# A sum of reciprocals on one core: every other early load issued by ScalarE, and fewer waits on VectorE

## The chip, the cores and the metric

One core of a Trainium2 chip. The metric is the time of one execution in device microseconds (us), as a median over several runs, with the kernel before measured beside each new one on the same chip. All runs compared here are undisturbed (fast). SyncE and ScalarE issue the loads; TensorE, VectorE, ScalarE and GpSimd (POOL in the profile) compute.

## The reference

```python
x = np.abs(np.random.randn(32, 512, 1024)).astype(np.float32) + 1e-6
return np.sum(1.0 / x, axis=-1).astype(np.float32)
```

That is 16,384 rows of 1024 numbers, 128 rows on each of 128 partitions, 67.11 MB to read and almost nothing to write. In what follows "row" means one row on each partition.

## The kernel before

The kernel never divides a single number. It splits each row in halves a and b and uses 1/a + 1/b = (a + b) / (a b). A product a b is made on GpSimd or, for some rows, on VectorE with b copied to PSUM by TensorE. ScalarE turns it into its reciprocal with Ln and Exp. VectorE multiplies by the other factor and sums: either over the whole row with the reciprocal broadcast, or over the sum a + b, which TensorE has made. Rows come in chunks of two, of three kinds `(rows, rows whose a + b TensorE makes, rows whose product VectorE makes)`:

```python
A, B, C = (2, 0, 0), (2, 2, 0), (2, 2, 1)
LOADS = [[A, B, A, C]] * 10 + [[A, B], [A, C]] * 4 + [[A], [B], [A], [C]] * 2
...
ppool = ctx.enter_context(tc.tile_pool(name="ppool", bufs=6))
...
def sum_row(c, row, fac):
    i = nc.vector.tensor_tensor_reduce(
        out=row, in0=row, in1=fac, scale=S, scalar=0.0, op0=mult, op1=plus,
        accum_out=sums[:, c : c + 1],
    )
...
for chunks in LOADS:
    n = sum(m for m, _, _ in chunks)
    xt = ring[:, c0 % R : c0 % R + n, :]                      # ring of R = 40 rows
    keep(nc.sync.dma_start(out=xt, in_=x_v[:, c0 : c0 + n, :]))
    # ... VectorE's products of this load
    # ... per chunk: GpSimd's product, TensorE's a + b,
    #     VectorE's sums of the chunk before, ScalarE's Ln and Exp
```

So the first ten loads have eight rows (4 MB) each, eight have four rows and eight have two. Each load needs ring rows that VectorE has done with.

## Time and profile before

| | |
|---|---|
| time before | 172.55 us (172.23 to 172.75, 4 runs) |
| span of the profiled run | 170.5 us |
| loads | 67.11 MB, near 425 GB/s from the second slice to the 37th |
| busiest engines | TensorE 80%, ScalarE 78%, GpSimd 78% |

The row of the DMA engines is full, the engines are not. One reads such a page by asking next how late each engine runs behind the loads, because the time ends with the last row's way through all of them. The lines for it are in the prediction.

### The profile page before, as it was taken

How to read it: one execution, taken by the hardware profiler on the slowest of the kernel's cores; microseconds unless marked ns; L12 is line 12 of the kernel's file. 1: busy time of each engine (PE TensorE's matmuls, PEld its weight loads, DVE VectorE, ACT ScalarE, POOL GpSimd, SP SyncE). 2: the span in 40 equal slices, each digit the busy share in tenths (PEclk: the TensorE clock that was granted, in tenths of full speed). 3: DMA queues.
4: the chain of work that ended last, by engine and by line, in shares of the span. 5: the costliest groups of instructions: out<-in, count | busy, mean ns of one | idle time of the engine just before them, and what ended most of it. 6: DMA issues, size and time to landing. Idle time of an engine off the chain costs nothing.

```text
span 170.5 us, 1320 instructions
## 1 busy us (share of the span) xinstructions
PE 136.0 (80%) x288; PEld 52.7 (31%) x288; DVE 124.9 (73%) x272; ACT 133.5 (78%) x129; POOL 133.0 (78%) x70
## 2 busy tenths in 40 slices
PE   0008999988889888786988887979999998896790
PEld 0003444332332333242333323323434332332240
DVE  0001778777987777787777769888998988889683
ACT  3002979979787997959799797899999988999790
POOL 1008969696996969589696969999999799996930
PEclk9999999999999999999999999999999999999999
DMA  6999999999999999999999999999999999999300
GB/s 208 415 446 431 438 423 446 415 454 423 448 423 431 431 438 419 431 432 423 446 415 446 423 404 427 431 423 431 427 427 423 427 413 423 421 421 419 146 0 15
DMA packets 3895, 67.25 MB, mean 394 GB/s; under 512 B 432, under 2 KB 560, under 8 KB 560
## 3 DMA queue, kind: packets, MB, share of 16 engines
q1 hardware_dynamic: 3888, 67.18, 92.7%
q8 instruction: 2, 0.03, 0.1%
q14 instruction: 5, 0.04, 0.1%
HBM read 67.11 MB, written 0.07 MB: 394 GB/s over the span
## 4 chain that ended last, share of the span: by engine, by line
DMA 66%; POOL 23%; issue 6%; DVE 1%; ACT 1%; DVEq 0%; POOLq 0%
DMA ring<-in_x_dram 66%; POOL pr L136 23%; DVE ring L92 1%; ACT pr L147 1%; ACT rc L151 1%; DVE pr L92 0%; DVEq L190 0%; POOLq L136 0%; DVE sums L92 0%; DVEq L92 0%
## 5 line engine op out<-in xcount | busy, mean ns | idle before, releaser
L136 POOL TENSOR_TENSOR pr<-ring 128x1024 f32<-128x1024 f32 x64 | 132.3, 2099 | 29.9 <-DMA ring<-in_x_dram 29.7
L82 PE MATMUL s<-ring,ident 128*128 128x512 f32 x256 | 121.2, 612 | 14.7 <-DVE sums L92 13.0
L92 DVE CUSTOM_DVE_ANT_1 ring<-ring,rc 128x1024 f32<-128x1024 f32 x64 | 75.6, 1219 | 26.2 <-ACT rc L151 22.2
L147 ACT ACTIVATE pr<-pr 128x1024 f32<-128x1024 f32 x64 | 67.3, 1051 | 30.0 <-POOL pr L136 29.7
L82 PEld LDWEIGHTS s<-ring,ident 128*128 128x128 f32 x256 | 47.4, 193 | 86.6 <-issue 49.4
L92 DVE CUSTOM_DVE_ANT_0 pr<-pr,s 128x512 f32<-128x512 f32 x64 | 41.4, 683 | 0.8 <-ACT pr L157 0.7
L157 ACT ACTIVATE pr<-pr 128x1024 f32<-128x1024 f32 x32 | 33.8, 1057 | 1.0
L151 ACT ACTIVATE rc<-pr 128x1024 f32<-128x1024 f32 x32 | 32.9, 1028 | 1.0
L82 PE MATMUL b<-ring,ident 128*128 128x512 f32 x32 | 18.5, 662 | 16.0 <-DMA ring<-in_x_dram 15.8
L125 DVE TENSOR_TENSOR pr<-ring,b 128x512 f32<-128x512 f32 x16 | 10.9, 684 | 16.1 <-PE b L82 16.0
L82 PEld LDWEIGHTS b<-ring,ident 128*128 128x128 f32 x32 | 5.3, 196 | 26.6 <-issue 15.4
L92 DVE DVE_READ_ACCUMULATOR2_ANT sums<- 128x1 f32 x128 | 10.6, 83 | 0.0
L53 ACT ACT_TABLE_LOAD x1 | 1.3, 1283 | 0.7 <-PEq L179 0.7
masks.py:197 POOL MEMSET ident<- 128x128 f32 x1 | 0.2, 204 | 0.3 <-POOLq L179 0.3
masks.py:199 POOL TENSOR_SCALAR_AFFINE_SELECT ident<-ident 128x128 f32<-128x128 f32 x1 | 0.3, 292 | 0.1
L179 POOL MEMSET const-float32-0.0<- 128x1 f32 x1 | 0.1, 98 | 0.2 <-issue 0.2
L179 POOL MEMSET const-bfloat16-1.0<- 128x1 bf16 x1 | 0.1, 101 | 0.0
L179 POOL MEMSET const-uint8-127<- 128x1 uint8 x1 | 0.1, 101 | 0.0
L179 POOL MEMSET const-float32-1.0<- 128x1 f32 x1 | 0.1, 98 | 0.0
## 6 DMA issues: line engine op xcount, KB each, us to landing
ring<-in_x_dram SPq DMA_DIRECT2D x10, 4096.0 KB, 37.7
ring<-in_x_dram SPq DMA_DIRECT2D x8, 2048.0 KB, 36.7
ring<-in_x_dram SPq DMA_DIRECT2D x8, 1024.0 KB, 28.2
out_dram<-sums SPq DMA_DIRECT2D x1, 64.0 KB, 1.5
```

What stands on the lines that cost most here:

```text
L53: nc.scalar.add_instruction(mybir.InstLoadActFuncSet(name=nc.get_next_instruction_name(), act_func_set_id=act_sets.index("natural_log_exp_ ...
L82: i = nc.tensor.matmul(bank, lhsT=ident, rhs=half, start=k == 0, stop=k == len(halves) - 1,)
L92: i = nc.vector.tensor_tensor_reduce(out=row, in0=row, in1=fac, scale=S, scalar=0.0, op0=mult, op1=plus, accum_out=sums[:, c : c + 1],)
L125: i = nc.vector.tensor_tensor(out=pr[:, j, :], in0=xt[:, q + j, :H], in1=b, op=mult)
L136: i = nc.gpsimd.tensor_tensor(out=pr[:, v:, :], in0=xc[:, v:, :H], in1=xc[:, v:, H:], op=mult)
L147: keep(nc.scalar.activation(out=pr, in_=pr, func=Ln, scale=S))
L151: i = nc.scalar.activation(out=rc, in_=pr[:, e:, :], func=Exp, scale=-1.0)
L157: keep(nc.scalar.activation(out=r, in_=r, func=Exp, scale=-1.0))
L179: nc = _bacc.Bacc("TRN2", target_bir_lowering=False, num_devices=1)
```

## The change

It has three parts. The loads 1, 3, 5, 7 and 9 are issued by ScalarE: two at the start, the others three loads ahead of the chunk that ScalarE is at. Every second of the ten big loads is A,B,A,B in place of A,B,A,C, which drops five products on VectorE and gives those rows to GpSimd. And VectorE is to wait less: the first sum of an A chunk writes its by-product to pr (the tile that holds the products) in place of the ring, the two rows of a B or C chunk are summed in reverse order, and pr gets two tags of four buffers.

```diff
-    LOADS = [[A, B, A, C]] * 10 + [[A, B], [A, C]] * 4 + [[A], [B], [A], [C]] * 2
+    LOADS = [[A, B, A, B], [A, B, A, C]] * 5 + [[A, B], [A, C]] * 4 + [[A], [B], [A], [C]] * 2
-    ppool = ctx.enter_context(tc.tile_pool(name="ppool", bufs=6))
+    ppool = ctx.enter_context(tc.tile_pool(name="ppool", bufs=4))
-    def sum_row(c, row, fac):
+    def sum_row(c, row, fac, out=None):
-            out=row,
+            out=row if out is None else out,
         # ... in sum_rows, for the rows of an A chunk:
+                pr[:, e : e + 2, :] if j == e and m - e > 1 else None,
-        for j in range(e):
+        for j in reversed(range(e)):
         # ... per load k, with AHEAD, OTHER = 3, 10:
-        keep(nc.sync.dma_start(out=xt, in_=x_v[:, c0 : c0 + n, :]))
+        ahead = range(k, k + AHEAD + 1) if k == 0 else (k + AHEAD,)
+        for a in ahead:
+            if a < OTHER and a % 2:
+                load(nc.scalar, a)
+        if k >= OTHER or k % 2 == 0:
+            load(nc.sync, k)
-            pr = ppool.tile([P, m, H], f32, tag="pr")
+            pr = ppool.tile([P, m, H], f32, tag="ps" if e else "pr")
```

More of the change, by code (lines that the diff above doesn't have):

```diff
@@ L33 @@
     F = 128
+    AHEAD, OTHER = 3, 10
     R = 40
@@ L107, in sum_rows, with load @@
             row = xc[:, j, :].rearrange("p (h e) -> p h e", h=2)
-            sum_row(c + j, row, rc[:, j - e, :].unsqueeze(1).to_broadcast([P, 2, H]))
-        for j in range(e):
-            sum_row(c + j, pr[:, j, :], sm[j])
+            sum_row(
+                c + j,
+                row,
+                rc[:, j - e, :].unsqueeze(1).to_broadcast([P, 2, H]),
+                pr[:, e : e + 2, :] if j == e and m - e > 1 else None,
+            )
+        for j in reversed(range(e)):
+            sum_row(c + j, pr[:, j, :], sm[j])
+    first = [0]
+    for chunks in LOADS:
+        first.append(first[-1] + sum(m for m, _, _ in chunks))
+    def load(eng, a):
+        r0, n = first[a], first[a + 1] - first[a]
+        i = eng.dma_start(
+            out=ring[:, r0 % R : r0 % R + n, :], in_=x_v[:, r0 : r0 + n, :]
+        )
+        keep(i)
     waiting = None
     c0 = 0
-    for chunks in LOADS:
+    for k, chunks in enumerate(LOADS):
         n = sum(m for m, _, _ in chunks)
         xt = ring[:, c0 % R : c0 % R + n, :]
-        keep(nc.sync.dma_start(out=xt, in_=x_v[:, c0 : c0 + n, :]))
+        ahead = range(k, k + AHEAD + 1) if k == 0 else (k + AHEAD,)
[4 more added lines that the diff above has]
+            load(nc.sync, k)
         made, q = [], 0
         for m, e, v in chunks:
-            pr = ppool.tile([P, m, H], f32, tag="pr")
+            pr = ppool.tile([P, m, H], f32, tag="ps" if e else "pr")
             for j in range(v):
```

## The prediction

> **What bounds the kernel now.** I read the page's first two parts, to see which resource is never idle.
>
> ```profile
> PE 136.0 (80%) x288; PEld 52.7 (31%) x288; DVE 124.9 (73%) x272; ACT 133.5 (78%) x129; POOL 133.0 (78%) x70
> DMA  6999999999999999999999999999999999999300
> GB/s 208 415 446 431 438 423 446 415 454 423 448 423 431 431 438 419 431 432 423 446 415 446 423 404 427 431 423 431 427 427 423 427 413 423 421 421 419 146 0 15
> ```
>
> No engine is above 80%, and the DMA row stands at 9 from the second slice to the 37th, at some 425 GB/s. The loads are the bound as long as they are queued early enough. That is in the part on DMA issues:
>
> ```profile
> ring<-in_x_dram SPq DMA_DIRECT2D x10, 4096.0 KB, 37.7
> ```
>
> A load lands 37.7 us after its issue while one takes about 9.85 us (first waits below: (102.11 - 13.42) / 9 loads), so nearly four loads are always queued. VectorE, which frees the ring, has that much slack and cannot starve the queue.
>
> Next the chain that ended last, in order of time, for what becomes of the two ends:
>
> ```profile
> 0.74 12.68 DMA ring<-in_x_dram
> ...
> 13.49 8.24 POOL pr L136 x4
> ...
> 64.52 37.59 DMA ring<-in_x_dram
> ...
> 131.56 25.52 DMA ring<-in_x_dram
> ...
> 159.69 2.38 POOL pr L136
> 162.09 1.07 ACT pr L147
> 163.18 1.04 ACT rc L151
> 164.34 0.62 DVE ring L92
> ```
>
> Load 0 lands at 13.42, load 9 at 102.11 (64.52 + 37.59). After the last loads a row goes through GpSimd's product, ScalarE's Ln and Exp and VectorE's sums; the output leaves at 167.95 and the span ends at 170.5. Last, the timeline of GpSimd alone, whose rows give start, length, and the wait before it:
>
> ```profile
> 23.18 8.27 POOL L136 TENSOR_TENSOR pr<-ring 128x1024 f32<-128x1024 f32 x4 [1.45 <-DMA ring<-in_x_dram]
> 102.27 32.99 POOL L136 TENSOR_TENSOR pr<-ring 128x1024 f32<-128x1024 f32 x16 [1.44 <-DMA ring<-in_x_dram]
> 157.24 6.21 POOL L136 TENSOR_TENSOR pr<-ring 128x1024 f32<-128x1024 f32 x3 [1.03 <-DMA ring<-in_x_dram]
> ```
>
> This is the view the prediction rests on. GpSimd needs 8.25 us per eight rows (32.99 / 4) against 9.85 of the loads: it waits 1.4 to 1.5 us for each big load and is one load behind the stream. From load 9 on the loads are smaller, and in 102.27 to 135.26 it works off that one load without a gap. It ends at 157.24 + 6.21 = 163.45. So **the slack of the compute side is small**: about 1.6 us a load, and it is nearly used up by the end.
>
> [...] The trace before has one queue for the loads, so no run shows it yet; my main step rests on it. [...] Here an issue on SP is 0.33 us in the median, and nothing waits for it. [...] the trace shows such a piece on VectorE's sequencer of 0.04 us in the final chain.
>
> **The change part by part.**
>
> *VectorE.* Five of the ten big loads change from A,B,A,C to A,B,A,B. Each drops one product on VectorE (684 ns in the groups by form, 5 x 0.684 = 3.4 us), two matmuls on b (592 ns at best) and the wait for them. The first sum of an A chunk writes into pr in place of the ring, and the two rows of B and C are summed in reverse, so that the first wait covers the second. I put this at some 0.05 us for each of 64 chunks, 3 us in all, by the 0.04 us above. VectorE is busy 73% and waits 22 us for ScalarE's Exp; all of this is **off the path**, except 0.1 to 0.2 us at the very end.
>
> *GpSimd.* It takes over those five rows. The forms are apart in the groups by line:
>
> ```profile
> L136 POOL TENSOR_TENSOR pr<-ring 128x1024 f32<-128x1024 f32 x48 | 112.6, 2372 | 29.8 <-DMA ring<-in_x_dram 29.7
> L136 POOL TENSOR_TENSOR pr<-ring 128x512 f32<-128x512 f32 x16 | 20.5, 1281 | 0.1
> ```
>
> A whole chunk is 2.37 us, a half 1.28: 1.09 us more in five loads, 5.5 us. An A,B,A,B load costs 8.25 + 1.09 = 9.34 us, nearly the 9.85 of a load. In one queue this alone would be hidden, since load 9 is of the old kind and GpSimd still waits before it.
>
> *pr in two tags of four.* A chunks lie two to a load, so four buffers reach back two loads, more than the six before did (a load and a half). No cost.
>
> *ScalarE issues loads 1, 3, 5, 7, 9.* Five issues at 0.33 to 1 us: some 2 us on an engine busy 78%. Their ring rows were freed before, since at iteration k it asks for the rows of load k - 2; so I expect no long wait there. The stream itself: SP holds loads 0, 2, 4 and ScalarE 1, 3 from the start. If the engines share, loads 0 and 1 move at half speed side by side. The stream's zero is 13.42 - 9.85 = 3.57, so both have landed by 3.57 + 19.7 = 23.3; with a head start of SP of about 1 us (ScalarE's table load, 1.28 us, comes first; an estimate) load 0 lands at about 22.6, load 1 at 24. **Compute starts 9 us later**, while the bytes per us stay the same. Pairs then land together: 2 and 3 at 42.3 and 43.7. ScalarE gets to the issue of load 5 only after its work on load 1, about 43; until the transfer starts[...] load 4 has the engines alone. So 4 and 5 land near 60 and 65.6, 6 and 7 near 79.4 and 85.3, 8 and 9 near 99 and 105. Some load is always queued: the stream ends as before.
>
> GpSimd from these, each load from the later of its landing and the end of the load before (9.34 for even, 8.25 for odd ones):
> load 0: 22.6 to 31.9; 1: to 40.2; 2: 42.3 to 51.6; 3: to 59.9; 4: to 69.2; 5: to 77.5; 6: 79.4 to 88.7; 7: to 97.0; 8: 99 to 108.4; 9: to 116.6.
> Before, load 9 was done at 102.27 + 8.25 = 110.5. The other 48 rows take 6 x 8.25 = 49.5 us: 116.6 + 49.5 = 166.1, against 163.45 before. They land before GpSimd gets to them, the last one at 162.06 (the b matmul's wait), where GpSimd would be ready for it at 164.9. So the tail is set by **GpSimd's backlog** in place of the last load, 166.1 - 163.45 = 2.65 us later. From there the tail is the same. Less 0.2 for VectorE's waits[...]: +2.2 us, 172.7 + 2.2 = 174.9 us.
>
> **The rivals.**
>
> *The stream gets faster.* Two queues could close gaps between packets. [...] Against it: the DMA share of the stretches is 1.00 to 1.02, so there are hardly gaps to close. [...] as the late start remains, it would land at 171 to 173 us.
>
> *The engines do not share, and take the loads in the order of issue.* Then nothing lands later, the 5.5 us on GpSimd hide, and it is 172.4 to 172.8.
>
> *ScalarE blocks.* If its issue waits for ring rows or a place in the queue, its Ln and Exp stop, and it has 8.1 us of work per load (1.04 + 1.03 per chunk, four chunks, less overlap). Against: SP issued all of the first five loads by 3.6 us without a wait. A block of 1 us at three issues would add up to 3 us: 176 to 178.
>
> *VectorE's waits matter after all.* They would if sums freed rows or PSUM banks too late. TensorE does wait 50 us for sums, but GpSimd does not. Gain 0.5 us at most.
>
> **Range and chances.** Sharing (some 75%) gives 173.5 to 176.5, its spread from the landings, which may be off by 1 us each; the other outcomes give 171 to 173. Hence 174.9, and 172.3 to 176.9 for 8 in 10. The 2% lines are 169.3 and 176.2: faster 0.03, as even the best stream leaves the late start; slower 0.18, for a longer start or a blocked ScalarE; same 0.79.
>
> **What would show it.** The first GpSimd product starting near 22.6 in place of 13.49, with two DMA queues carrying 46 and 21 MB (SP 88 rows of 128, ScalarE 40); GB/s still some 425 and ending near 160; GpSimd busy 138 us, and without gaps from about 99 us to an end near 166; the final chain made of GpSimd in place of DMA over its last third. A first product before 16 us, or a stream above 432 GB/s throughout, would make the prediction wrong.

Where the marks stand, passages are cut that no trace or run of this case shows. That two queues share the DMA engines ("it" in "no run shows it yet"), the runs below measure. With the second, and in the first rival, went a limit of 2% on what a second queue could gain, which rested on a top rate that is not shown; so the 171 to 173 us of that rival are no more than the author's estimate. In the trace before the best ten us ran at 437 GB/s and 13.42 to 102.11 us at 431. (Its DMA share was 0.99 to 1.02 in the stretches that were asked for between 13.4 and 157 us.) The "piece" of 0.04 us is the one at 164.22 us in the chain. Two terms of the forecast, no measurement behind them: 1.6 us from ScalarE's issue to the start of its transfer, which is contained in the landings of loads 4 to 9 and so in the 166.1, and 0.3 us taken off for a better stream. The sum came to 2.65 - 0.2 - 0.3 = 2.15, given as +2.2 us, hence 174.9. Its 0.2 is the author's estimate from the 0.04 us.

## The result, and the profile after

The changed kernel takes 173.76 us (173.53 to 173.88, 4 runs) beside 172.55 us before. The ratio is 1.0070, with a 95% interval of 1.0049 to 1.0091. Ratios here are the mean time of one kernel's fast runs over that of the other's of the same rounds, so not quite the ratio of the medians.

First the page of the changed kernel: the engines, the DMA row, the two queues of the loads (packets, MB, share), and the chain that ended last.

```profile
PE 129.5 (75%) x278; PEld 51.0 (30%) x278; DVE 121.9 (71%) x267; ACT 133.3 (77%) x129; POOL 138.0 (80%) x70
DMA  6999999999999999999999999999999999999000
...
q1 hardware_dynamic: 3168, 46.20, 63.5%
q10 hardware_dynamic: 720, 20.97, 28.3%
...
DMA 44%; ACT 25%; POOL 13%; issue 9%; DVE 7%; SPq 0%; POOLq 0%; DVEq 0%; ACTq 0%
```

The DMA row is as full as before, and 21 MB go through the second queue. GpSimd has 5 us more to do. The chain is no longer mostly loads: after the wait for load 8 at 97.3 us it runs through GpSimd, ScalarE and VectorE until 113.8, and from there to the end through ScalarE and, from 153, VectorE. In that last third GpSimd (10.00 us busy in every ten up to 160) and ScalarE (9.7 to 9.8 in every ten from 120 on) are both full, so which of the two is on the chain says little.

Do the engines share? ScalarE issues load 5 at 42.65 us. Here are the DMA queues from 42.8 to 46.0 us, and then from 46 to 50:

```profile
q1 hardware_dynamic: 41, 1.34, 97.2%
```

```profile
q10 hardware_dynamic: 28, 0.92, 53.2%
q1 hardware_dynamic: 26, 0.85, 49.4%
```

Until 46.0 load 4 has the engines alone; as soon as load 5 moves, each queue gets about half of the engines' time (53.2% and 49.4%). Next GpSimd's timeline (start, length, and the wait before it), which answers to the one in the prediction:

```profile
23.14 17.53 POOL L159 TENSOR_TENSOR pr<-ring 128x1024 f32<-128x1024 f32 x8 [21.83 <-DMA ring<-in_x_dram]
42.63 35.10 POOL L159 TENSOR_TENSOR pr<-ring 128x1024 f32<-128x1024 f32 x16 [1.97 <-DMA ring<-in_x_dram]
78.14 9.35 POOL L159 TENSOR_TENSOR pr<-ring 128x1024 f32<-128x1024 f32 x4 [0.41 <-DMA ring<-in_x_dram]
87.66 8.29 POOL L159 TENSOR_TENSOR pr<-ring 128x1024 f32<-128x1024 f32 x4 [0.18 <-DMA ring<-in_x_dram]
97.42 66.99 POOL L159 TENSOR_TENSOR pr<-ring 128x1024 f32<-128x1024 f32 x32 [1.47 <-DMA ring<-in_x_dram]
```

By the semaphore events load 0 is there at 23.06 us and load 1 at 23.24; GpSimd starts at 23.14, 9.65 us later than before. Loads 2 and 3 come together too (42.49 and 42.67). Load 8 is what the wait at 97.42 is for; before, GpSimd began it here:

```profile
92.55 8.28 POOL L136 TENSOR_TENSOR pr<-ring 128x1024 f32<-128x1024 f32 x4 [1.45 <-DMA ring<-in_x_dram]
```

From 97.42 GpSimd works 66.99 us without a gap and ends at 164.41, against 163.45 before: 0.96 us later. The end of the span moved by 1.6 us (170.5 to 172.1), so some 0.6 us more were lost after GpSimd's end, 0.4 of it before the output is issued (at 169.31, before at 167.95). The timeline of ScalarE in the changed kernel shows where:

```profile
165.70 1.06 ACT L170 ACTIVATE pr<-pr 128x1024 f32<-128x1024 f32 x1 [0.24 <-DVE pr L148]
```

The last Ln waits for VectorE's product of the last C chunk, which in VectorE's order stands behind sums that also run late now; it was done at 165.6, and before at 163.9.

### The profile page after: what moved, and what is told of

It reads as the page before. It is cut to its first block, busy times and chain, and to the rows that moved or that the text cites. A ratio compares the mean times of both kernels' runs of the same rounds, so it can differ in the third digit from the quotient of the medians.

```text
span 172.1 us, 1264 instructions
## 1 busy us (share of the span) xinstructions
PE 129.5 (75%) x278; PEld 51.0 (30%) x278; DVE 121.9 (71%) x267; ACT 133.3 (77%) x129; POOL 138.0 (80%) x70
## 3 DMA queue, kind: packets, MB, share of 16 engines
q1 hardware_dynamic: 3168, 46.20, 63.5%
q10 hardware_dynamic: 720, 20.97, 28.3%
## 4 chain that ended last, share of the span: by engine, by line
DMA 44%; ACT 25%; POOL 13%; issue 9%; DVE 7%; SPq 0%; POOLq 0%; DVEq 0%; ACTq 0%
DMA ring<-in_x_dram 44%; ACT pr L170 15%; POOL pr L159 13%; ACT pr L180 6%; ACT rc L174 4%; DVE pr L93 3%; DVE ring L93 3%; DVE pr L148 1%; DVE sums L93 0%; SPq L124 0%; POOLq L159 0%; DVEq L93 0%; ACTq L170 0%; DVEq L213 0%
## 5 line engine op out<-in xcount | busy, mean ns | idle before, releaser
L159 POOL TENSOR_TENSOR pr<-ring 128x1024 f32<-128x1024 f32 x64 | 137.2, 2206 | 25.9 <-DMA ring<-in_x_dram 25.9
L83 PEld LDWEIGHTS s<-ring,ident 128*128 128x128 f32 x256 | 46.9, 193 | 109.3 <-issue 71.9
L93 DVE CUSTOM_DVE_ANT_1 pr<-ring,rc 128x1024 f32<-128x1024 f32 x32 | 39.1, 1221 | 47.3 <-ACT rc L174 47.3
L93 DVE CUSTOM_DVE_ANT_1 ring<-ring,rc 128x1024 f32<-128x1024 f32 x32 | 38.9, 1217 | 0.0
L83 PE MATMUL b<-ring,ident 128*128 128x512 f32 x22 | 11.3, 595 | 0.0
L148 DVE TENSOR_TENSOR pr<-ring,b 128x512 f32<-128x512 f32 x11 | 7.5, 683 | 0.0
L83 PEld LDWEIGHTS b<-ring,ident 128*128 128x128 f32 x22 | 4.1, 190 | 5.4 <-issue 4.8
```

The source lines that it names most:

```text
L83: i = nc.tensor.matmul(bank, lhsT=ident, rhs=half, start=k == 0, stop=k == len(halves) - 1,)
L93: i = nc.vector.tensor_tensor_reduce(out=row if out is None else out, in0=row, in1=fac, scale=S, scalar=0.0, op0=mult, op1=plus, accum_out ...
L148: i = nc.vector.tensor_tensor(out=pr[:, j, :], in0=xt[:, q + j, :H], in1=b, op=mult)
L159: i = nc.gpsimd.tensor_tensor(out=pr[:, v:, :], in0=xc[:, v:, :H], in1=xc[:, v:, H:], op=mult)
```

## The experiments

All have the correct result and were timed in five rounds. They were run in three sessions on three chips, where the kernel before took 172.35, 172.28 and 172.38 us (172.55 in the comparison above); across sessions the ratios to it compare better than the times.

### One queue

My theory was that GpSimd's backlog comes of the late pairs and the extra rows together, so that without the second queue the extra rows cost nothing.

```diff
-    AHEAD, OTHER = 3, 10
+    AHEAD, OTHER = 3, 0        # and so all loads on SyncE
```

> The changed kernel with all loads back on SyncE's queue; the ten big loads keep their five extra rows on GpSimd and VectorE keeps its new sums. Theory (loads landing in late pairs, with GpSimd's extra rows, leave a backlog): the first product starts near 13.5, GpSimd needs 9.34 us for the new kind of load and 9.85 us are there, so it still waits before load 9, ends near 163.4 and the time is 172.2 to 172.7, as before the change. Rival (the five extra rows, 5.5 us of GpSimd, cost time by themselves): 173.5 or more.

It took 171.89 us (171.66 to 172.09), ratio 0.9973 (0.9960 to 0.9986). The rival falls. The version is even faster than the kernel before, by 0.3%, which neither theory had. **The second queue costs about 1.9 us** (173.76 against 171.89; 1.7 us by the two ratios). GpSimd's timeline in it:

```profile
92.73 9.34 POOL L159 TENSOR_TENSOR pr<-ring 128x1024 f32<-128x1024 f32 x4 [1.44 <-DMA ring<-in_x_dram]
102.80 32.94 POOL L159 TENSOR_TENSOR pr<-ring 128x1024 f32<-128x1024 f32 x16 [0.73 <-DMA ring<-in_x_dram]
```

GpSimd still waits for loads 8 and 9. Its five extra rows are hidden.

### Two queues with the rows of before

```diff
-    LOADS = [[A, B, A, B], [A, B, A, C]] * 5 + ...
+    LOADS = [[A, B, A, C]] * 10 + ...
```

> The changed kernel with the two queues, but with A,B,A,C in all ten big loads as before. Theory (only both together cost): the last pair lands near 97.4 and 104.5 as in the changed kernel, GpSimd works 97.4 to 113.9 on it, then 49.5 us more: end near 163.4, time 172.4 to 172.9. Rival (two queues or a late start cost by themselves, by slower transfers or by ScalarE's time of issue): 173.5 or more, or a stream that ends later than 160.

It took 174.23 us (174.06 to 174.90), ratio 1.0117 (1.0103 to 1.0132). **My theory fell here**: without the extra rows the second queue costs as much or slightly more. Its GpSimd timeline, last two groups:

```profile
79.44 16.49 POOL L159 TENSOR_TENSOR pr<-ring 128x1024 f32<-128x1024 f32 x8 [2.84 <-DMA ring<-in_x_dram]
98.87 65.83 POOL L159 TENSOR_TENSOR pr<-ring 128x1024 f32<-128x1024 f32 x32 [2.93 <-DMA ring<-in_x_dram]
```

GpSimd waits nearly 3 us before each of these pairs; here it is not behind the loads, the loads are behind it. Load 8 comes 1.45 us later than in the changed kernel. With less work on GpSimd, ScalarE reaches its issues earlier (load 5 at 41.64 in place of 42.65 us, load 9 at 78.58 in place of 79.71), and by the semaphore events of the two traces loads 4, 6 and 8 land 1.7, 1.3 and 1.5 us later, loads 5, 7 and 9 1.5, 1.0 and 0.4 us earlier. That fits queues which share the engines for longer; the shares themselves were read in the changed kernel only. For load 8 this is more than the 1.09 us that its lighter work saves. GpSimd ends at 98.87 + 65.83 = 164.70.

The new theory: what counts is when load 8 lands, since from there GpSimd has 64 rows to do, some 66 us. In the kernel before it had room: 92.55 + 66 = 158.5 against its end at 163.45, so 4.9 us of lateness would have been free. The pairs use up 4.87 us (97.42 - 92.55) and the heavier load 8 another 1.09.

### A late start in one queue

```diff
-    AHEAD, OTHER = 3, 10
+    AHEAD, OTHER = 3, 0
-    LOADS = [[A, B, A, B], [A, B, A, C]] * 5 + ...
+    LOADS = [[A, B, A, B, A, B, A, C]] + [[A, B, A, B], [A, B, A, C]] * 4 + ...
```

> One queue, GpSimd's extra rows kept, and the first two big loads made one load of sixteen rows, so that the first product starts near 23.3 as in the changed kernel, but everything after it lands one by one. Theory (not the late start alone but the later pairs hold GpSimd up, as it waits again at 42.6, 78, 87.7 and 97.4): GpSimd works without a gap from 23.3 until near 111 us, has caught up with the stream and ends near 163.4: 172.2 to 172.8. Rival (the nine us of late start are the whole cost): 173.5 or more.

It took 171.64 us (171.51 to 171.83), ratio 0.9961 (0.9949 to 0.9973). That is even below the range of the theory, as the version with one queue was. GpSimd's timeline, the first two of its lines with products:

```profile
23.25 112.35 POOL L159 TENSOR_TENSOR pr<-ring 128x1024 f32<-128x1024 f32 x52 [21.95 <-DMA ring<-in_x_dram]
136.49 4.70 POOL L159 TENSOR_TENSOR pr<-ring 128x1024 f32<-128x1024 f32 x2 [0.89 <-DMA ring<-in_x_dram]
```

GpSimd starts as late as in the changed kernel, works 112 us without a gap, and has caught up with the loads by 136. **The late start costs nothing.** What costs is to be made to wait again later.

### ScalarE until load 5 only

```diff
-    AHEAD, OTHER = 3, 10
+    AHEAD, OTHER = 3, 6
```

> The changed kernel with ScalarE issuing only loads 1, 3 and 5; loads 7 and 9 go back to SyncE. Theory (what counts is when the last pair of big loads lands: load 8 at 97.4 in place of near 92.5, with 64 rows still to do): the first product starts near 23.1 all the same, but from load 6 on the loads land one by one as before, GpSimd works off its backlog, and the time is 171.6 to 172.2, as with one queue. Rival (the late start, or issues on ScalarE as such): 173 or more.

It took 171.77 us (171.65 to 171.92), ratio 0.9969 (0.9957 to 0.9981), with 12.58 MB still on the second queue. Late start, two queues and issues on ScalarE are all there; only the last two pairs are gone. It is as fast as with one queue. So none of the three costs by itself. GpSimd never waits again after loads 2 and 3, and ends 1.8 us earlier than in the changed kernel, at 42.73 + 119.89 = 162.62:

```profile
42.73 119.89 POOL L159 TENSOR_TENSOR pr<-ring 128x1024 f32<-128x1024 f32 x56 [1.95 <-DMA ring<-in_x_dram]
```

### ScalarE for load 9 only

```diff
-            if a < OTHER and a % 2:
+            if a == 9:
...
-        if k >= OTHER or k % 2 == 0:
+        if k != 9:
```

> The changed kernel with ScalarE issuing only load 9, three loads ahead; the nine others on SyncE. Theory (two queues share the engines and a load issued early takes its share from the loads that are needed first): start near 13.5 as before, load 9 lands ahead of load 8, which comes only near 102 by the same recurrence, with 64 rows still to do: GpSimd ends near 168 to 169 and the time is some 5 us up, 175.5 to 178. Rival (no sharing to speak of with one load, or the cost is that of five issues or of the late start): 171.7 to 172.6.

It took 178.18 us (178.14 to 178.43), ratio 1.0343 (1.0330 to 1.0356), just above the range of the theory. Against the version with one queue, one single load on the other queue costs 6.3 us, where five cost 1.9. GpSimd's last three groups:

```profile
72.64 9.34 POOL L159 TENSOR_TENSOR pr<-ring 128x1024 f32<-128x1024 f32 x4 [2.00 <-DMA ring<-in_x_dram]
86.01 8.27 POOL L159 TENSOR_TENSOR pr<-ring 128x1024 f32<-128x1024 f32 x4 [4.03 <-DMA ring<-in_x_dram]
101.79 66.95 POOL L159 TENSOR_TENSOR pr<-ring 128x1024 f32<-128x1024 f32 x32 [7.51 <-DMA ring<-in_x_dram]
```

Load 9, issued at 72.62, overtakes: loads 7 and 8 come 3 and 9 us later than in one queue, as they would if it takes its share of the engines from them (the shares were not read in this run). In the trace load 9 is complete at 99.3 and load 8 at 101.7. The end is 101.79 + 66.95 = 168.74, 5.3 us after that of the kernel before, and the time is up by 5.9. The same 66 to 67 us from load 8 to GpSimd's end hold in this run, in the changed kernel and in the one with the rows of before. The lower granted clock of TensorE in these runs (0.955 to 0.968) is thus no rival: GpSimd needs 66.95 us here and 66.99 in the changed kernel. One thing beside the theory: ScalarE's issue of this load took 3.26 us in place of 0.33, and its next Ln came about 0.9 us late; why is not shown.

### The old sums with two queues

```diff
-                pr[:, e : e + 2, :] if j == e and m - e > 1 else None,
+                None,
-        for j in reversed(range(e)):
+        for j in range(e):
```

> The changed kernel with VectorE's sums as before (all A sums written back into the ring, rows of B and C in forward order), two queues and new rows kept. Theory (VectorE's waits are off the path but for the last chunk): 173.6 to 174.0, at most 0.3 over the changed kernel. Rival (the new sums won back about a microsecond of the loss): 174.7 or more.

It took 173.90 us (173.60 to 174.83), ratio 1.0098 (1.0079 to 1.0117), beside 1.0070 for the changed kernel. The median is 0.14 us higher (0.5 us by the ratios, as the two were run in different sessions), and the intervals overlap. With the late pairs the new sums are worth at most about half a microsecond, and perhaps nothing.

### The sums alone, and the rows alone

Two runs were to say what made the version with one queue faster than the kernel before. The first is that version with A,B,A,C in all ten loads; the second is the kernel before with the new rows.

```diff
-    LOADS = [[A, B, A, B], [A, B, A, C]] * 5 + ...       # first: one queue, new sums
+    LOADS = [[A, B, A, C]] * 10 + ...
```

> The kernel before with the new sums and the two pr tags only (one queue, A,B,A,C in all ten). It says which part made the one-queue version faster than the kernel before by 0.27%. If the sums did it: 171.7 to 172.0. If the rows did it: 172.3 to 172.6.

> The kernel before with the five new rows only (A,B,A,B in every second big load, one queue, old sums, six pr buffers). If the rows made the one-queue version faster: 171.7 to 172.0. If the sums did: 172.3 to 172.6, since GpSimd's 5.5 us are hidden behind the loads.

The sums alone took 171.87 us (171.79 to 171.93), ratio 0.9975 (0.9962 to 0.9988): **this part of the change made it faster by 0.4 us** (the new sums and the two pr tags, which no run takes apart). With the new rows as well it was 171.89. The rows alone took 172.99 us, but in two clusters: 172.23, 172.28 and 172.54, as the kernel before, and 173.44, 173.66 and 173.79. The slow ones had a TensorE clock of 0.98 to 0.99, but so had one of the fast (0.99 at 172.54). The profile is of a slow one, and in it the granted clock (0.50, the third figure from the end) fell to half just when TensorE made the last sums. The window from 163.4 to 166.8 us, the last eight matmuls and VectorE's wait for them in this run, and then those matmuls in the kernel before:

```profile
163.40:166.80 3.40, 3.40 (x6) 1.34 (x5) 2.86 (x4) 3.10 (x4) 0.29 (x1) 0.50 0.00 0
163.27 5.29 PE L82 MATMUL s<-ring,ident 128*128 128x512 f32 x8
168.72 0.69 DVE L92 CUSTOM_DVE_ANT_0 pr<-pr,s 128x512 f32<-128x512 f32 x1 [1.10 <-PE s L82]
```

```profile
163.03 3.60 PE L82 MATMUL s<-ring,ident 128*128 128x512 f32 x8
```

That wait is 1.1 of the some 1.4 us by which this run (173.79) is above the fast ones; the other two slow runs have no profile. The fast cluster says that the rows cost nothing there.

How can the sums help a kernel that its loads bound? TensorE's timeline tells when the last load is there, in the kernel before and in that with the new sums alone:

```profile
162.06 1.13 PE L82 MATMUL b<-ring,ident 128*128 128x512 f32 x2 [1.17 <-DMA ring<-in_x_dram]
```

```profile
161.22 1.13 PE L83 MATMUL b<-ring,ident 128*128 128x512 f32 x2 [1.16 <-DMA ring<-in_x_dram]
```

The last load itself comes 0.84 us earlier. The queue was full in both (the DMA row stands at 9 in every slice from 138 to about 158 us), so it is unlikely that waits on VectorE did that by freeing the ring. The DMA queues in the window from 138 to 163 us, again for the kernel before and for the sums alone:

```profile
q1 hardware_dynamic: 1196, 8.85, 85.0%
q14 instruction: 1, 0.01, 0.1%
```

```profile
q1 hardware_dynamic: 1198, 8.88, 85.2%
```

In the kernel before an instruction fetch runs there, at 154.1 us in the trace, when VectorE is at its 325th instruction of 362. That it is VectorE's is inferred: in every run with such a fetch, it comes at VectorE's 317th to 329th instruction. The new sums have 330 in all (with the new rows 320), and the fetch comes after the loads, at 163.6, or not at all.

### More instructions, same waits

To part the fetch from the waits, the one-queue version got memsets of one element on VectorE before any load has landed, forty in one kernel and sixty-six in the other.

```diff
+    pad = opool.tile([P, 1], f32)
+    for _ in range(40):                 # 66 in the second kernel
+        keep(nc.vector.memset(pad, 0.0))
```

> The one-queue version (changed sums and rows, 171.89 us) with forty one-element memsets on VectorE at its start, before any load has landed; nothing else changes, and all its waits are as before. In the kernel before, an instruction fetch runs at 154.1 us, at VectorE's 325th instruction, and the last loads land 0.7 us later than in the versions with the new sums, whose VectorE has fewer instructions and fetches after the loads or not at all. Theory (the fetch among the last loads is what the new sums took away): the fetch comes at some 150 to 158 us, the last load lands near 161.6 in place of 161.0, time 172.3 to 172.6. Rival (the waits as such): 171.8 to 172.0.

> The same with sixty-six memsets, which puts the fetch near 140 to 146 us. If a fetch costs only among the last small loads: 171.8 to 172.1. If any fetch beside the loads costs the end 0.5 us: 172.3 to 172.6. If instructions at the start delay anything: the first product would start later than 13.6.

With forty: 173.01 us (172.65 to 173.34), ratio 1.0029 (1.0005 to 1.0053). With sixty-six: 173.07 us (172.60 to 174.14), ratio 1.0035 (1.0006 to 1.0063). Both lose about 1.1 us against the 171.89 without them, more than the gain of the sums. The memsets were over at 5.75 and 9.0 us, and the first product started at 13.45 with forty and 13.81 with sixty-six, beside 13.64 without. By the ratios the losses are 1.0 and 1.1 us (the chips differ). The last load in TensorE's timeline of the kernel with forty, whose fetch came at 155.0 us:

```profile
162.32 1.12 PE L83 MATMUL b<-ring,ident 128*128 128x512 f32 x2 [1.18 <-DMA ring<-in_x_dram]
```

That is 0.83 us later than the 161.49 of the version without memsets. In the one with sixty-six the fetch came at 142.6 and the last load at 162.10, so a fetch need not stand among the very last loads. So the gain of the sums is most likely not their waits: with the same waits and 360 instructions, beside the 362 of the kernel before, it is gone. That the fetch is the link is likely, since each of the four kernels with such a fetch between 142 and 159 us (the rows alone had theirs at 158.4) got its last load after 162.0, and the one-queue versions with fewer instructions at 161.1 to 161.5.

The traces of three of the four say more. Each load has 16 semaphore events, which I take as one for each of the 16 DMA engines. In the kernel before, the last of the 16 comes 2.2 us after the first for the load that is there at 153.7, and 3.1 us for the next one, during which the fetch runs; so too with forty memsets (2.35, then 3.3, fetch at 155.0) and with the rows alone (2.25, then 3.05, fetch at 158.4). With the sums alone it stays at 2.1. The first event of the last load comes at about the same time with the fetch and without (158.94 and 159.07), so it is not the stream as a whole that comes late; I take that as a sign against a wait for ring rows. With sixty-six it does not fit as well: there the 1.9 us grow to 2.7 by 137.2, before the fetch at 142.6, and by only 0.3 with it. The link is not shown in isolation: the memsets may have moved other fetches too, which was not taken apart, and the loss is larger than I expected (1.0 to 1.1 us, where 0.4 to 0.7 were expected of the forty).

## Why the prediction was right or wrong

The time of 173.76 lies in the range of 172.3 to 176.9, and the class is "same", as given 0.79. The change was forecast as +2.2 us and measured as +1.2. The errors below have both signs (GpSimd's end 1.7 us too late, the tail 0.6 us too short), so a part of the agreement is luck.

**The bound, right.** The stream was full and stayed so, at the same rate; the 0.3 us that the sum took off for a better stream were not there (422 to 435 GB/s in each 20 us from 20 to 140 before, 424 to 433 after). The last load did land earlier, at 161.1 in place of 162.0 us, but so it does in the one-queue versions with the new sums (161.1 to 161.4).

**Sharing of the engines, right.** The first product came at 23.14, foreseen near 22.6; the queues carried 46.20 and 20.97 MB and had about half of the engines' time each from 46 to 50 us (49.4% and 53.2%); no first load landed early. Loads 0 and 1 were 0.2 us apart, not the 1.4 of the assumed head start.

**"Compute starts 9 us later" as the cause, wrong.** The start is late, but the run with one load of sixteen rows shows that it is worked off. The step that counts was in the list of landings all along: the last pair. The runs with ScalarE until load 5 and with load 9 only show that alone.

**The 5.5 us of extra rows in the backlog, wrong.** In the sum they seemed to be part of what the backlog is made of. With two queues and no extra rows the time is 174.23, and with one queue they cost nothing (171.89 and 171.87). Only the heavier load 8 comes after the last wait, 1.09 us, and the extra work also delays ScalarE's issues, which helps load 8 by 1.45 us.

**The size: "8 and 9 near 99 and 105", mis-sized.** Load 8 was there for GpSimd at 97.42 and GpSimd ended at 164.41, not at 166.1. This term is off by 1.6 to 1.7 us. The step that failed in it is "until the transfer starts", for which the forecast took 1.6 us: load 5 was issued at 42.65 and its first packet moved at 46.1, 3.5 us later, and so long load 4 had the engines alone (97.2% of their time). In that stretch load 4 moves at the full rate in place of about half (49.4% from 46 to 50 us), so each microsecond more of it brings load 4, and SyncE's loads behind it, one microsecond earlier: 1.9 us by this estimate, 1.7, 1.4 and 1.7 measured (loads 4, 6 and 8 at 58.3, 78.0 and 97.3, foreseen at 60, 79.4 and 99). Loads 7 and 9 were issued at 62.18 and 79.71 us, before 5 and 7 had landed (67.10 and 87.53), so nothing of this kind came later.

**"From there the tail is the same", wrong by 0.6 us.** All engines are near full by then (TensorE 9.9, VectorE 9.5, ScalarE 9.7 and GpSimd 10.0 us busy from 150 to 160), and the last product on VectorE stood behind late sums. The sign "the final chain made of GpSimd in place of DMA over its last third" failed too: that third runs through ScalarE and VectorE, with GpSimd full beside them.

**"Less 0.2 for VectorE's waits", too small, and by another way.** The sums are worth 0.4 us in one queue, and the forty memsets speak against the waits as the reason. With two queues they are worth 0.14 us by the medians and 0.5 by the ratios, with intervals that overlap.

The balance: the second queue costs 1.7 to 1.9 us in its full form, the new sums give back about 0.4 of a microsecond against the kernel before, the new rows are hidden. The versions with one queue (171.89), with sums alone (171.87), with a first load of sixteen rows (171.64) and with ScalarE until load 5 (171.77) all beat both kernels. They lie too close together to choose among them.

## What to carry to other kernels

In this kernel, bound by its loads, the second queue did not move bytes faster (422 to 435 GB/s with one, 424 to 433 with two, from 20 to 140 us); it changed the order in which they land, and a load issued early took its share from one that was needed first (with load 9 alone on ScalarE, GpSimd began load 8 at 101.79 us in place of 92.73, and the time was 6.3 us longer). Compare the landing of the last big loads with the work that is still to do after them: here a start 9.6 us later cost nothing (171.64 us), since GpSimd had caught up with the loads by 136 us. And an edit that seems to save waits may work by other things that it changes: here forty memsets of one element took 1.0 to 1.1 us with the waits of the program as they were, more than the new sums had gained. So take the wait and the count apart before giving the credit.
